# Value products of two heads issued alternately, and transpositions branch by branch, in a two-layer HGRN2 / NSA block

## The chip, the cores and the metric

One core of a Trainium2 chip runs the whole block in one launch. The metric is the device time of one execution in microseconds (us), the median of several runs; lower is better.

## The reference

The input x has 256 tokens of 1024 features. Layer 0 is an HGRN2 mixer and a gated feed-forward; layer 1 is a native sparse attention (NSA) mixer and another feed-forward, each with conditioning vectors (shift, scale, gate) made from c. The change touches the last step of the NSA mixer: for each head three softmaxes (compressed keys, selected blocks, window) are multiplied with their values, gated and added.

```python
p_c = masked_softmax(s_c, cmp_end[None, :] <= t[:, None])
o_c = jnp.einsum('bhgqc,bchd->bqhgd', p_c.astype(vc.dtype), vc)
...
p_s = masked_softmax(s_s, m_s[:, :, None])
o_s = jnp.einsum('bhgqk,bhqkd->bqhgd', p_s.astype(vs_g.dtype), vs_g)
...
p_w = masked_softmax(s_w, m_w)
o_w = jnp.einsum('bhgqk,bkhd->bqhgd', p_w.astype(vw.dtype), vw)
...
o = g[:, :, 0] * o_c + g[:, :, 1] * o_s + g[:, :, 2] * o_w
```

There are 16 query heads of 64 features on 4 key heads. With 256 tokens every block is selected and the window holds all earlier tokens, so selection and window are both causal attention over 256 keys, with keys and values of their own.

## The kernel before

All weights come as one stream of 1 MB chunks (`SCHED`, line 116), loaded by SP into a ring of four buffers (`raw`, lines 282 to 289). Most chunks are split into a high and a low fp32r part, `wh` on ACT and `wl` on DVE (lines 307 and 308), and each product is three matmuls of these parts (lines 484 to 486). Conditioning chunks are read by PE as they are (L385, tiles `adapsg` and `adapsss`).

The NSA stage works on eight column tiles j; a tile holds two heads, one on partitions 0 to 63 (half 0) and one on 64 to 127 (half 1). Tiles 0 to 3 belong to group g = 0, tiles 4 to 7 to g = 1. `attend_scores` (line 1195) makes scores on PE (`s`, L1207), adds the mask and takes maxima on DVE (L1211), exponentials on ACT (L429), reciprocals with gates on DVE (`cf`, L1223 to L1225), and scales the probabilities `Pt[half]` on DVE (L1229). For each half and each branch (br 0 selection, br 1 window) there are three blocks of 128 x 128: keys 0 with tokens 0, keys 0 with tokens 1, keys 1 with tokens 1.

`attend_values` (line 1233) transposes the three blocks of each half and branch on PE (`ptt`, L1244), copies them to SBUF (`PT[half, br]`; the first on DVE, L1247, the other three on ACT, L1249), and then sums the products with the values into one accumulator `po`. Half 0 writes its partitions 0 to 63 and half 1 its partitions 64 to 127, which are two column halves of the PE array (`tile_position=(0, 64 * half)`). For each half there are five products: compressed probabilities `PC` with `VC` over 256 tokens (L1256), and for each branch keys 0 over 256 tokens (L1260) and keys 1 over the last 128 (L1262). Before, all five of half 0 come first, then the five of half 1. Operands are plain fp32, and each such matmul is two instructions on the engine. At the end `split` (L479 on ACT, L480 on DVE) makes the parts `hh` and `hl` of the output projection's input (`nso`).

The same array halves are used by the compression products of line 1103 (tile `cmp`), which take the two kinds in turn, and the conditioning products of L385 use four column quarters.

The order of the work is `ORDER["nsa"]` (line 66): scores s, values v and conditioning chunks a are interleaved there. A tile scheduler then places the instructions by expected readiness and priority; `attend_values` is moved ahead by ten places (`@first("av")`, `PRI`). So the rows of one tile's step do not stand together in PE's queue, and other work stands between them. PSUM gives three buffers to `ptt` (tag `acc`, shared with the projections) and four to `po`, scores and others (tag `m`); `PT` has five buffers in SBUF.

Of the kernel before, what the change touches and what calls it, by code (L numbers as in the profile page):

```python
# [20 lines left out]
P = 128  # L21
S = 256
D = 1024
# [4 lines left out]
RAW = 4  # chunks loaded ahead  # L28
DEFER = 3  # chunks of a feed-forward's first product taken before rstd is there
XBUFS = 14  # L30
XMOD, XOFF = 5, 9  # every how many halves of a chunk go to the second ring, and until which chunk
PTS = 3  # pairs of heads with probabilities at a time
QACT, KACT = 0x0F, 0xF0  # chunks of the queries' and values' input made on ACT
CSTK = 7  # chunk after which the rest of the constants is loaded
# how far ahead of the program (behind it, if negative) some of the work is issued
PRI = {"gates": -100, "av": 10, "res": 60, "rot": -15, "fh": 60}
EPS = 1e-6
# [5 lines left out]


# conditioning vectors (s shift and scale, g gate) on the tensor engine; the others are row sums on DVE
# [11 lines left out]
# The order of the work. hgrn: D decays, S scores, i/g products, V values. nsa: q queries, G gates, c compression,  # L57
# n norms, w values, x compressed softmax, s scores, v outputs, a conditioning chunk.
# hada, f0, f1: after how many chunks of products each conditioning chunk comes.
# [115 lines left out]
def row_constants():  # L175
    """Row 32 m + h of column block m: ones on the partitions of half h."""
    r = np.zeros((P, 4, P), np.float32)
    for m in range(4):
        for h in range(2):
            r[32 * m + h, m, 64 * h:64 * h + 64] = 1.0  # L180
    return r.reshape(P, 4 * P)


def first(name):
    """What the method issues is moved by PRI in the order of the program."""
    def wrap(f):
        def g(self, *a, **k):
            n = PRI.get(name, 0)
            if not n:
                return f(self, *a, **k)  # L190
            with self.tc.high_priority(offset=n):
                return f(self, *a, **k)
        return g
    return wrap


class K:
# [154 lines left out]
    def ada(self, kind, l, i, t):  # L352
        """Two columns of 128 conditioning values: rows of the chunk against c."""
        nc = self.nc
        m, A, bias = self.ada_tiles(l)
        c0, c1 = (i, 8 + i) if kind == "ada_ss" else (16 + 2 * i, 17 + 2 * i)
        for h, c in enumerate((c0, c1)):
            junk = self.tp.tile([P, D], F32, tag="junk", bufs=1, name="junk")
            nc.vector.tensor_tensor_reduce(out=junk, in0=t[:, h * D:(h + 1) * D], in1=self.crep, scale=1.0,  # L359
                                           scalar=0.0, op0=ALU.mult, op1=ALU.add, accum_out=m[:, c:c + 1])  # L360
        if kind == "ada_ss":
            gain = self.col(self.gain(l))
            nc.vector.scalar_tensor_tensor(A[:, i:i + 1], m[:, c1:c1 + 1], self.bias1(l)[:, c1:c1 + 1],
                                           gain[:, i:i + 1], op0=ALU.add, op1=ALU.mult)
            nc.vector.tensor_tensor(m[:, i:i + 1], m[:, i:i + 1], bias[:, i:i + 1], op=ALU.add)
            if i == 7:
                self.mods[("A", l)] = A
                self.mods[("shift", l)] = m[:, 0:8]
        else:
            nc.vector.tensor_tensor(m[:, c0:c1 + 1], m[:, c0:c1 + 1], bias[:, c0:c1 + 1], op=ALU.add)  # L370
            if i == 3:
                self.mods[("gate", l)] = m[:, 16:24]

    def ada_pe(self, kind, l, i, t):
        """c against the chunk's rows, summed over the chunks; at the last one the columns."""
# [43 lines left out]
    def act(self, out, in_, func, **kw):  # L419
        """An activation whose function lies in a table set; sets change only between phases."""  # L420
# [17 lines left out]
    def rsqrt_cols(self, v, n, tag):  # L438
        """v ** -0.5 for a few columns, by Newton's method from the exponent."""
# [11 lines left out]
    def rsqrt(self, v, shape, tag):  # L451
        """(v + EPS) ** -0.5, one Newton step after the tables."""
# [13 lines left out]
    def sigmoid(self, out, v, shape):  # L466
        """exp(min(v, 0)) / (1 + exp(-|v|))"""
        nc = self.nc
        t = self.s2.tile(shape, F32, tag="sg", bufs=1, name="sg")
        nc.vector.tensor_scalar_min(t, v, 0.0)  # L470
        self.act(t, t, AF.Exp)
        nc.scalar.activation(out, v, AF.Abs)
        self.act(out, out, AF.Exp, scale=-1.0)
        nc.vector.tensor_scalar_add(out, out, 1.0)
        nc.vector.reciprocal(out, out)
        nc.vector.tensor_tensor(out, out, t, op=ALU.mult)
# [17 lines left out]
    def gemm(self, ps, w, hh, hl, n=256):  # L494
        """ps = sum over k of w[k] (128 x 128) against h[:, k, :n]."""
# [3 lines left out]
    def tiles(self, w):  # L499
        """The 128 x 128 tiles of half a chunk: high and low parts."""  # L500
# [7 lines left out]
    def set_shift(self, hh, hl, l):  # L508
        """Columns 256 and 257 of the moving operand: the shift vector and zeros."""
# [14 lines left out]
    def stat(self, x, m):  # L524
        """Adds the squares of chunk m to the sum over chunks."""
# [10 lines left out]
    def first_stat(self):  # L536
        """rstd of the input."""
# [25 lines left out]
    def stat_end(self, ps=None):  # L563
        """self.rstd = (mean of squares + EPS) ** -0.5 of every token, on all partitions."""
# [17 lines left out]
    def full_chunk(self, hh, hl, m, A, sh, pool):  # L582
        """Chunk m of x * rstd * A + shift, in two parts."""
# [7 lines left out]
    def full_pair(self, which, l, xr, pool, on_act):  # L591
        """The same from x * rstd."""
# [22 lines left out]
    def gemm_deferred(self, ws, h, pool, name, ub=2):  # L615
        """Products with h as it is before rstd: their values times rstd, and the shift's column."""
# [17 lines left out]
    def residual(self, ps, m, gate, nxt):  # L634
        """x_new chunk m = x + gate * y, with what the next products need of it."""
# [20 lines left out]
    def hgrn(self):  # L656
# [3 lines left out]
        with self.tc.tile_pool(name="hg", bufs=1) as gp, self.tc.tile_pool(name="hg2", bufs=2) as g2:  # L660
# [17 lines left out]
            # room of the next operands until their first parts are there  # L678
# [62 lines left out]
    def gemm_tok(self, ps, h, ws):  # L741
        """Tokens on the partitions: h (stationary) against the weights."""
# [9 lines left out]
    def hgrn_decays(self, fs, qs, g2):  # L752
        """X[l]: exp of the log decay from each block's middle; left keys, right queries. X[8]: keys."""
# [41 lines left out]
    def hgrn_scores(self, X, q, g2, i):  # L795
        nc = self.nc
        # scores inside blocks of 32, all levels side by side
# [45 lines left out]
    def hgrn_values(self, ns, As, v, g2, q):  # L843
        """Into q: rms-normalised rows of A^T v times the gain, features on the partitions."""
# [75 lines left out]
    def raw_heads(self, ps, name):  # L920
        """Products of two column tiles off the accumulator, and their squares."""
# [7 lines left out]
    def rotate(self, u, gain, swap, kr, name):  # L929
        """kr = the rotation of u times the gain: halves of a head change places."""  # L930
# [11 lines left out]
    def head_norm(self, pairs, kr, gain=None, kn=None):  # L942
        """Four column tiles: kr times the heads' rstd, kn = u times that and the gain."""
        nc = self.nc
        ps = self.m_tile([P, S], "hs")
        # rows 32 e and 32 e + 1: the two heads of column tile e
# [124 lines left out]
    def cmp_blocks(self, sw, u, kind, Dt, pool):  # L1071
        """Dt[(parity, d), i, (head, block)]: token 16 block + 2 i + parity of a head, plus its position."""
# [160 lines left out]
    def attend_values(self, j):  # L1233
# [4 lines left out]
        for half in range(2):  # L1238
            for br in range(2):
                PT[half, br] = self.pt_tile(f"PT{j}_{half}{br}")  # L1240
                pt = self.pp.tile([P, 3, P], F32, tag="acc", bufs=3, name="ptt")
                # columns: keys 0 with tokens 0, keys 0 with tokens 1, keys 1 with tokens 1
# [8 lines left out]
        for half in range(2):  # L1251
            hs = slice(64 * half, 64 * half + 64)
            kv = 2 * g + half
            o = po[hs]
            tpos = (0, 64 * half)
            nc.tensor.matmul(o, lhsT=self.VC[:, g, (j % 4) * 2 + half], rhs=self.PC[g].rearrange("p a b -> p (a b)"),  # L1256
                             start=True, stop=False, tile_position=tpos)
            for br in range(2):
                v = self.V[:, :, br, 64 * kv:64 * kv + 64]
                nc.tensor.matmul(o, lhsT=v[:, 0], rhs=PT[half, br][:, 0:S], start=False, stop=False,  # L1260
                                 tile_position=tpos)
                nc.tensor.matmul(o[:, P:S], lhsT=v[:, 1], rhs=PT[half, br][:, S:384], start=False, stop=br == 1,  # L1262
                                 tile_position=tpos)
# [6 lines left out]
def _kt(w):  # L1270
    """[K, M] -> [128, K / 128, M]"""
# [3 lines left out]
def head_order():  # L1275
    """Query heads by (column tile, half): halves of a tile use key heads 2 g and 2 g + 1."""
# [107 lines left out]
```

## Time and profile before

| what | us |
|---|---|
| median of 3 runs | 765.33 (764.39 to 766.17) |
| profiled execution: span, first to last instruction | 764.0 |
| median of the runs less that span | 1.3 |
| PE busy / weight loads / DVE / ACT, of the span | 736.8 / 671.6 / 573.1 / 395.2 |
| all transpositions, value products and what stands between them | 474 to 546 of the span |

The page gives for each engine the time in which it had at least one instruction under way. PE's matmuls overlap each other and their ends are modelled, so for PE the distance between the starts of two rows says what an instruction took. In a timeline, rows of one kind that follow each other are merged: start, length of the merged row, engine, line, operation, tiles, shape and count.

### The profile page before, as it was taken

What the parts mean: (1) busy time and instruction counts of PE and PEld (TensorE: products, weight loads), DVE (VectorE), ACT (ScalarE), POOL (GpSimd) and SP (SyncE); (2) the same over time, 40 slices, a digit from 0 to 9 for tenths busy, and PEclk for the clock granted to TensorE, in tenths of its full rate; (3) what the DMA queues carried; (4) which work ended last, traced back from release to release, by engine and by line L of the source; (5) the groups of instructions that cost most, each with busy time, mean ns of one, the idle gap of its engine ahead of it and who ended that gap; (6) DMA issues with size and microseconds to landing.
All of it is one profiled execution on the core that took longest, in us unless ns stands there. A gap on an engine that the chain in (4) does not pass through costs nothing.

```text
span 764.0 us, 15991 instructions
## 1 busy us (share of the span) xinstructions
PE 736.8 (96%) x6580; PEld 671.6 (88%) x6580; DVE 573.1 (75%) x1231; ACT 395.2 (52%) x746; POOL 0.6 (0%) x7
## 2 busy tenths in 40 slices
PE   3999999899999999999999899999999999999997
PEld 1999986689999999999996787555799999999997
DVE  5996988469898988987598869668489757565631
ACT  4339856357644544544474644558466444444330
POOL 0000000000000000000000000000000000000000
PEclk9999999799999999999999999999999999999999
DMA  8999745475489796887733942552755555755710
GB/s 330 335 341 355 274 133 210 139 284 203 143 320 377 275 366 266 333 333 285 274 112 97 359 134 74 173 215 109 275 204 182 208 179 206 275 203 205 266 39 21
DMA packets 26571, 174.13 MB, mean 228 GB/s; under 512 B 3201, under 2 KB 4609, under 8 KB 6018
## 3 DMA queue, kind: packets, MB, share of 16 engines
q1 hardware_dynamic: 24912, 170.80, 60.7%
q10 hardware_dynamic: 1586, 2.32, 1.1%
q8 instruction: 51, 0.84, 0.4%
q14 instruction: 22, 0.18, 0.1%
HBM read 170.48 MB, written 1.05 MB: 225 GB/s over the span
## 4 chain that ended last, share of the span: by engine, by line
PE 88%; DVE 5%; ACT 3%; DMA 2%; issue 1%; ACTq 0%; DVEq 0%
PE ff L486 11%; PE ff L485 11%; PE ff L484 11%; PE ffo L484 6%; PE ffo L485 5%; PE ffo L486 5%; PE adapsss L385 2%; PE po L1260 2%; PE ptt L1244 2%; PE s L1207 2%; DVE wl L308 1%; PE q L485 1%; PE nso L484 1%; PE hg_i L748 1%; PE hgo L484 1%; PE q L486 1%
## 5 line engine op out<-in xcount | busy, mean ns | idle before, releaser
L308 DVE TENSOR_TENSOR wl<-raw,wh 128x1024 fp32r<-128x1024 f32 x201 | 244.0, 1222 | 72.7 <-ACT wh L307 72.2
L307 ACT CAST wh<-raw 128x1024 fp32r<-128x1024 f32 x201 | 208.7, 1048 | 152.8 <-PE ff L485 53.0
L486 PE MATMUL ff<-hh,wl 128*128 128x256 f32 (+1 forms) x704 | 198.3, 282 | 0.0
L484 PE MATMUL ff<-hh,wh 128*128 128x256 f32 (+1 forms) x704 | 198.1, 282 | 0.0
L485 PE MATMUL ff<-hl,wh 128*128 128x256 f32 (+1 forms) x704 | 198.1, 282 | 0.0
L486 PEld LDWEIGHTS ff<-hh,wl 128*128 128x128 f32 x704 | 133.1, 189 | 0.0
L485 PEld LDWEIGHTS ff<-hl,wh 128*128 128x128 f32 x704 | 132.7, 189 | 0.3
L484 PEld LDWEIGHTS ff<-hh,wh 128*128 128x128 f32 x704 | 132.6, 189 | 0.1
L484 PE MATMUL ffo<-gh,wh 128*128 128x256 f32 x352 | 99.0, 282 | 0.6 <-DVE x L638 0.6
L485 PE MATMUL ffo<-gl,wh 128*128 128x256 f32 x352 | 98.6, 280 | 0.0
L486 PE MATMUL ffo<-gh,wl 128*128 128x256 f32 x352 | 98.5, 280 | 0.0
L359 DVE CUSTOM_DVE_ANT_0 junk<-raw,crep 128x1024 f32<-128x1024 f32 x64 | 78.1, 1220 | 2.8 <-DMA raw<-in_w 2.2
L484 PEld LDWEIGHTS ffo<-gh,wh 128*128 128x128 f32 x352 | 66.0, 188 | 1.3 <-DVE x L638 1.0
L486 PEld LDWEIGHTS ffo<-gh,wl 128*128 128x128 f32 x352 | 66.1, 188 | 0.0
L485 PEld LDWEIGHTS ffo<-gl,wh 128*128 128x128 f32 x352 | 66.1, 188 | 0.0
L479 ACT CAST gh<-fg 128x256 fp32r<-128x256 f32 x44 | 17.8, 405 | 42.0 <-DVE fg L894 41.4
L429 ACT ACTIVATE Pt<-Pt,nm 128x128 f32<-128x128 f32 x64 | 28.2, 442 | 9.8 <-DVE nm L1215 9.8
L480 DVE TENSOR_TENSOR gl<-fg,gh 128x256 fp32r<-128x256 f32 x44 | 18.6, 422 | 8.2 <-ACT gh L479 8.2
L587 ACT ACTIVATE hh<-t,mod 128x256 fp32r<-128x256 f32 x24 | 11.4, 505 | 24.6 <-DVE t L586 24.6
L429 ACT ACTIVATE fs<-ff 128x256 f32<-128x256 f32 x38 | 14.5, 380 | 15.3 <-PE ff L486 15.3
L638 DVE SCALAR_TENSOR_TENSOR x<-ffo,mod,x 128x256 f32<-128x256 f32 x16 | 7.7, 482 | 18.9 <-PE ffo L486 18.9
L385 PE MATMUL adapsss<-raw,c 128*32 128x512 f32 x128 | 21.1, 632 | 0.8 <-issue 0.8
(324 smaller groups left out, 1497.8 us busy)
## 6 DMA issues: line engine op xcount, KB each, us to landing
raw<-in_w SPq DMA_DIRECT2D x160, 1024.0 KB, 5.6
x<-in_x SPq DMA_DIRECT2D x2, 512.0 KB, 5.0
usq<-huq ACTq DMA_DIRECT2D x16, 64.0 KB, 2.4
out<-x SPq DMA_DIRECT2D x8, 128.0 KB, 1.9
cst<-in_cst ACTq DMA_DIRECT2D x1, 558.0 KB, 7.7
usk<-huk ACTq DMA_DIRECT2D x8, 64.0 KB, 3.9
raw<-in_w SPq DMA_DIRECT2D x1, 512.0 KB, 4.3
rselr<-in_rsel SPq DMA_DIRECT2D x1, 256.0 KB, 2.9
```

Source lines behind the costliest of these rows:

```text
L307: nc.scalar.copy(wh, u)
L308: nc.vector.tensor_tensor(wl, u, wh.bitcast(F32), op=ALU.subtract)
L359: nc.vector.tensor_tensor_reduce(out=junk, in0=t[:, h * D:(h + 1) * D], in1=self.crep, scale=1.0, scalar=0.0, op0=ALU.mult, op1=ALU.add, a ...
L385: nc.tensor.matmul(self.aps[32 * j:32 * j + 32, :q], lhsT=self.c32[:, k], rhs=t[:, n * D + j * q:n * D + (j + 1) * q], start=k == 0, stop= ...
L429: r = nc.scalar.activation(out, in_, func, **kw)
L479: self.nc.scalar.copy(hi, v)
L480: self.nc.vector.tensor_tensor(lo, v, hi.bitcast(F32), op=ALU.subtract)
L484: mm(ps, lhsT=wh, rhs=hh, start=first, stop=False)
L485: mm(ps, lhsT=wh, rhs=hl, start=False, stop=False)
L486: mm(ps, lhsT=wl, rhs=hh, start=False, stop=last)
L1207: nc.tensor.matmul(ps, lhsT=self.QR[hs, j, tt * P:tt * P + P], rhs=self.KR[hs, g, :, 0:n], start=True, stop=True)
L1244: nc.tensor.transpose(pt[:, e], Pt[half][:, br, e * P:(e + 1) * P], self.c("ident"))
```

## The change

The two nested loops over half and branch change places where the blocks are transposed: both halves of branch 0 first, then both of branch 1. And the ten value products go step by step, each step for half 0 and then half 1, in one statement (L1261 in the changed program, for L1256, L1260 and L1262 before). The first step opens the sum (`start`), the last closes it. The products themselves, their operands, shapes and places in the array are as before. The rest of the diff takes out comments and docstrings.

```diff
-        for half in range(2):
-            for br in range(2):
+        for br in range(2):
+            for half in range(2):
                 PT[half, br] = self.pt_tile(f"PT{j}_{half}{br}")
...
         po = self.m_tile([P, S], "po")
-        for half in range(2):
-            hs = slice(64 * half, 64 * half + 64)
-            kv = 2 * g + half
-            o = po[hs]
-            tpos = (0, 64 * half)
-            nc.tensor.matmul(o, lhsT=self.VC[:, g, (j % 4) * 2 + half], rhs=self.PC[g].rearrange("p a b -> p (a b)"),
-                             start=True, stop=False, tile_position=tpos)
-            for br in range(2):
-                v = self.V[:, :, br, 64 * kv:64 * kv + 64]
-                nc.tensor.matmul(o, lhsT=v[:, 0], rhs=PT[half, br][:, 0:S], start=False, stop=False,
-                                 tile_position=tpos)
-                nc.tensor.matmul(o[:, P:S], lhsT=v[:, 1], rhs=PT[half, br][:, S:384], start=False, stop=br == 1,
-                                 tile_position=tpos)
+
+        pc = self.PC[g].rearrange("p a b -> p (a b)")
+        steps = [(None, self.VC[:, g, (j % 4) * 2:(j % 4) * 2 + 2], pc, slice(0, S))]
+        for br in range(2):
+            for e, t in ((0, slice(0, S)), (1, slice(P, S))):
+                steps.append((br, self.V[:, e, br, P * g:P * g + P].rearrange("p (h d) -> p h d", h=2),
+                              slice(0, S) if e == 0 else slice(S, 384), t))
+        for n, (br, w, r, t) in enumerate(steps):
+            for half in range(2):
+                rhs = r if br is None else PT[half, br][:, r]
+                nc.tensor.matmul(po[64 * half:64 * half + 64, t], lhsT=w[:, half], rhs=rhs, start=n == 0,
+                                 stop=n == len(steps) - 1, tile_position=(0, 64 * half))
         self.split(self.O[0][:, j, :256], self.O[1][:, j, :256], po)
```

On PE, the block in which tile 2's products stand complete (tile 3's first ones ahead of them and among them). In `PT_01` the first digit is the half, the second the branch; 64x256 and 64x128 are what a product writes.

```order
-L1256 MATMUL po<-PC_5655,VC 64x256 x2
-L1260 MATMUL po<-PT_00_6249,V 64x256
-L1262 MATMUL po<-PT_00_6249,V 64x128
-L1260 MATMUL po<-PT_01_6255,V 64x256
-L1262 MATMUL po<-PT_01_6255,V 64x128
-L1256 MATMUL po<-PC_5655,VC 64x256
-L1260 MATMUL po<-PT_10_6261,V 64x256
-L1262 MATMUL po<-PT_10_6261,V 64x128
-L1260 MATMUL po<-PT_11_6267,V 64x256
-L1262 MATMUL po<-PT_11_6267,V 64x128
+L1261 MATMUL po<-PC_5655,VC 64x256 x4
+L1261 MATMUL po<-PT_00_6249,V 64x256
+L1261 MATMUL po<-PT_10_6255,V 64x256
+L1261 MATMUL po<-PT_00_6249,V 64x128
+L1261 MATMUL po<-PT_10_6255,V 64x128
+L1261 MATMUL po<-PT_01_6261,V 64x256
+L1261 MATMUL po<-PT_11_6267,V 64x256
+L1261 MATMUL po<-PT_01_6261,V 64x128
+L1261 MATMUL po<-PT_11_6267,V 64x128
```

Half 0 and half 1 now alternate row by row; tile 3's product of half 1 with `PC` came to this block from the next one. Of the four rows with `PC` the first two are half 0 of tiles 2 and 3, the last two half 1.

Also on PE, in the changed program, the products of tile 6 and the last transpositions of tile 7 (`Pt_0_6557` and `Pt_1_6558`, halves 0 and 1), with the numbers of the buffers:

```order
L1261 MATMUL po_6627<-PT6_00_6603,V_4885 64x256
L385 MATMUL adapsss3_6426<-raw117_6437,c32_110 32x512 x3
L385 MATMUL adapsss3_6426<-raw118_6601,c32_110 32x512 x4
L385 MATMUL adapsss3_6426<-raw119_6644,c32_110 32x512 x4
L1261 MATMUL po_6688<-PC1_6382,VC_5474 64x256
L1261 MATMUL po_6627<-PT6_10_6609,V_4885 64x256
L1261 MATMUL po_6627<-PT6_00_6603,V_4885 64x128
L1244 MATMUL ptt_6665<-cst_80,Pt7_0_6557 128x128
L1261 MATMUL po_6627<-PT6_10_6609,V_4885 64x128
L1261 MATMUL po_6627<-PT6_01_6615,V_4885 64x256
L1244 MATMUL ptt_6665<-cst_80,Pt7_0_6557 128x128 x2
L1261 MATMUL po_6627<-PT6_11_6621,V_4885 64x256
```

Here the scheduler has put other work between the two halves of a step: `PT6_00` stands alone ahead of eleven conditioning products, and `PT6_01` is parted from `PT6_11` by transpositions.

On ACT, the copies of tile 1 among the steps of the query norm (`hry`, `hrt`):

```order
 L1249 COPY PT_11_6065<-ptt 128x384
-L1249 COPY PT_01_6090<-ptt 128x384
+L1249 COPY PT_10_6090<-ptt 128x384
 L429 ACTIVATE hry<-hry 128x256
-L1249 COPY PT_10_6096<-ptt 128x384
+L1249 COPY PT_01_6096<-ptt 128x384
+L459 ACTIVATE hrt<-hry 128x256
 L1249 COPY PT_11_6102<-ptt 128x384
-L459 ACTIVATE hrt<-hry 128x256
```

The two middle copies carry the other pair of half and branch, and the square `hrt` now goes before the last copy of tile 1.

## Rows read from the trace of the kernel before

**Rows 1.** From the page: the span, and the shares of the chain that ended last by engine.

```profile
span 764.0 us, 15991 instructions
...
PE 88%; DVE 5%; ACT 3%; DMA 2%; issue 1%; ACTq 0%; DVEq 0%
```

**Rows 2.** Busy time by stretch: stretch and its length, then busy us and instructions of PE, weight loads, DVE, ACT and POOL, the granted clock of PE, the share of the DMA engines, GB/s.

```profile
475.00:546.00 71.00, 70.49 (x459) 39.22 (x460) 46.56 (x209) 40.72 (x140) 0.00 (x0) 1.00 0.50 189
546.00:600.00 54.00, 53.80 (x443) 53.09 (x444) 46.38 (x88) 33.76 (x61) 0.00 (x0) 1.00 0.54 185
```

**Rows 3.** The chain of waits in the window 460 to 560 us: shares of this window by engine, tile and line (the row is cut by the view).

```profile
by line: PE po L1260 14.3%; PE ptt L1244 13.3%; PE s L1207 12.3%; PE adapsss L385 9.5%; ACT Pt L429 7.1%; PE po L1262 6.5%; PE po L1256 6.0%; PE nso L484 5.1%; PE nso L486 4.6%; PE nso L485 4.5%; PE adapsg L385 3.4%; DVE Pt L1211 2.4%; PE c
```

**Rows 4.** The matmuls that write the tile `po`: count, durations (least, median, most, in ns), first and last start, form (the part of the array, the moving operand).

```profile
L1260 PE MATMUL po<-PT,V x64: 379/379/430, 479.6 to 545.3; 128*64 128x256 f32 x64
L1262 PE MATMUL po<-PT,V x64: 272/273/323, 480.1 to 545.6; 128*64 128x128 f32 x64
L1256 PE MATMUL po<-PC,VC x32: 379/379/431, 475.9 to 544.2; 128*64 128x256 f32 x32
```

**Rows 5.** The timeline of PE from 497.4 to 501.0: the block of the first listing above.

```profile
497.48 1.08 PE L1256 MATMUL po<-PC,VC 128*64 128x256 f32 x4
498.40 0.59 PE L1260 MATMUL po<-PT,V 128*64 128x256 f32 x2
498.83 0.38 PE L1262 MATMUL po<-PT,V 128*64 128x128 f32 x2
499.05 0.38 PE L1260 MATMUL po<-PT,V 128*64 128x256 f32 x1
499.05 0.43 PE L1256 MATMUL po<-PC,VC 128*64 128x256 f32 x1
...
499.48 0.27 PE L1262 MATMUL po<-PT,V 128*64 128x128 f32 x1
...
500.19 0.59 PE L1260 MATMUL po<-PT,V 128*64 128x256 f32 x2
500.62 0.38 PE L1262 MATMUL po<-PT,V 128*64 128x128 f32 x2
500.93 0.44 PE L396 MATMUL adat<-cst,adasm 128*128 128x128 f32 x2
```

**Rows 6.** The timeline of the compression products, 416.2 to 424: weight loads and matmuls.

```profile
416.32 6.67 PEld L1103 LDWEIGHTS cmp<-raw,D 128*64 128x64 f32 x62
416.32 7.12 PE L1103 MATMUL cmp<-raw,D 128*64 128x256 f32 x62
```

**Rows 7.** The timeline of PE from 473 to 547: where blocks of products and their neighbours begin.

```profile
479.60 0.65 PE L1260 MATMUL po<-PT,V 128*64 128x256 f32 x2
...
481.53 1.91 PE L385 MATMUL adapsg<-raw,c 128*32 128x256 f32 x26
...
484.18 0.65 PE L1260 MATMUL po<-PT,V 128*64 128x256 f32 x2
...
487.41 1.20 PE L1244 MATMUL ptt<-cst,Pt 128*128 128x128 f32 x9
488.55 1.07 PE L385 MATMUL adapsg<-raw,c 128*32 128x256 f32 x16
489.55 0.51 PE L959 MATMUL hb<-hry,rsel 128*128 128x256 f32 x2
...
506.61 0.65 PE L1260 MATMUL po<-PT,V 128*64 128x256 f32 x2
...
509.19 1.20 PE L1244 MATMUL ptt<-cst,Pt 128*128 128x128 f32 x9
```

**Rows 8.** Groups of instructions on ACT, 475 to 546: count, busy us, mean ns of one, idle time before them and what ended it.

```profile
L429 ACT ACTIVATE Pt<-Pt,nm 128x128 f32<-128x128 f32 (+1 forms) x48 | 21.1, 443 | 4.8 <-DVE nm L1215 4.8
...
L1249 ACT COPY PT<-ptt 128x384 f32<-128x384 f32 x24 | 10.5, 478 | 11.1 <-PE ptt L1244 10.5 <-ACT wh L307 0.6
```

**Rows 9.** Who waited for whom, 475 to 546: us in total, times, longest.

```profile
ACT PT L1249 <- PE ptt L1244: 10.5, 7, 4.6
ACT hh L479 <- PE po L1262: 9.6, 5, 3.1
...
DVE Pt L1211 <- PE s L1207: 3.1, 5, 1.1
...
PEld ptt L1244 <- DVE cf L1223: 1.6, 2, 0.8
```

**Rows 10.** The same view, 546 to the end.

```profile
ACT wh L307 <- PE ff L485: 34.1, 25, 1.8
```

**Rows 11.** Busy time by stretch, columns as in rows 2.

```profile
520.00:525.00 5.00, 5.00 (x20) 2.10 (x19) 4.59 (x25) 5.00 (x24) 0.00 (x0) 1.00 0.13 51
530.00:535.00 5.00, 5.00 (x35) 2.34 (x37) 4.58 (x12) 4.96 (x21) 0.00 (x0) 1.00 0.00 0
```

**Rows 12.** The same view, ahead of the stage of the change.

```profile
405.00:410.00 5.00, 3.30 (x17) 2.46 (x18) 5.00 (x10) 2.00 (x5) 0.00 (x0) 0.83 0.22 41
410.00:415.00 5.00, 5.00 (x36) 4.87 (x36) 4.17 (x13) 2.62 (x8) 0.00 (x0) 0.83 0.69 236
445.00:450.00 5.00, 3.27 (x25) 3.06 (x24) 4.96 (x13) 2.17 (x3) 0.00 (x0) 0.92 0.01 3
450.00:455.00 5.00, 5.00 (x34) 5.00 (x34) 4.36 (x6) 1.05 (x2) 0.00 (x0) 0.74 0.60 202
```

## The prediction

> **What bounds the kernel now.** I read the head of the page first: the span is 764.0 us and TensorE (PE) makes 88% of the chain of work that ended last [rows 1]. So an edit is worth what it takes off PE's queue in a stretch where PE is the chain. The edit touches only the products `po` and the transpositions `ptt`, which stand between 475 and 546 us; the busy time by stretch shows PE taken for 70.5 of those 71 us at full clock (1.00 in the clock column is the 2.4 GHz level), with DVE at 47 and ACT at 41 [rows 2]. A busy PE in this profile may still be a slow PE, since its matmuls overlap, so I went on to the chain of waits of the window 460 to 560. That window is 100 us long, so a per cent is a microsecond: the three lines of the products hold 14.3 + 6.5 + 6.0 = **26.8 us** [rows 3]. They are 160 instructions (each matmul of the program with fp32 operands is two on the engine): 96 over 256 columns and 64 over 128 [rows 4].
>
> **What such a product costs.** The timeline of one block, tiles 2 and 3, shows it [rows 5]. Distances between starts are what counts; the durations in the rows overlap. Four products of one half start at 497.48 and the next group at 498.40: 0.92 us, which is 4 x 0.216 and 0.05 for the change of the array's shape. Two over 128 columns take 499.05 - 498.83 = 0.22, so 0.109 each. The last two start at 500.62 and the next work, of another shape, at 500.93: 0.31, two times 0.109 and 0.09 for the change back. A piece of products between other work thus costs its stream and 0.05 + 0.09, some 0.15.
>
> At 499.05 two rows start together: L1260 of half 0 and L1256 of half 1. They write different column halves of the array and run side by side. The kernel has a stage that does this all along: the compression products of L1103 are issued alternately for column halves 0 and 64, and 62 of them take 7.12 us [rows 6]; the last one's own 0.38 taken off, that is 61 steps in 6.74 us, 0.110 each, half of 0.216. It is the same shape (128 rows, 64 columns, 256 moving columns, fp32). So **two halves side by side cost as much as one**, and the edit makes the products stand in that order.
>
> Here a rule of the Trainium skill speaks against the change: "TensorE: Matmul & The Clock Gate", Part 3, says that a load of weights overlaps a matmul in flight only where the two use different rows of the array, and that matmuls start strictly in program order. Both halves here use all 128 rows, so by it alternation would win nothing (rival 2). The trace disagrees: 62 loads go beside 62 products in the compression [rows 6], and L1256 at 499.05 started ahead of L1262 at 499.48, which the program issues before it.
>
> **Products, after.** Not every second can be won, since the halves overlap in part already and a scheduler places the rows. In the order of the program before, half 1's first product stands four engine instructions behind the place where it started [rows 5], so I let a product start as soon as the one four places ahead has started, and its own half is free. One row of the order is 0.43 us (256 columns) or 0.22 (128). Down the order of the changed program, stream and 0.15 for each piece:
> - Tiles 0 and 1: twice two rows of the same half, 1.01 each; then 00, 10, 00, 10, 01: 0.43 + 0.22 + 0.43 + 0.15 = 1.23; then eleven rows, half 1 the longer with 1.95: 2.10.
> - Tiles 2 and 3: twelve rows, all in pairs: 2.16 + 0.15 = 2.31; then eight in pairs: 1.45.
> - Tiles 4 and 5: 1.01, 1.01, 0.58, 0.37 (scores and transpositions stand between), ten rows 1.87, four 0.79, and a single one, 0.58.
> - Tiles 6 and 7: 0.58, 0.79, 0.58, 0.58, 0.37, 0.58, 0.58, and seven rows 1.45.
>
> These 21 pieces are 20.8 us. Before, the same stretch has the 26.8 of the chain; as a check on the method, the pieces of tiles 0 to 3 before take 1.93 (479.60 to 481.53), 3.23 (484.18 to 487.41), 3.45 (497.48 to 500.93) and 2.58 (506.61 to 509.19) [rows 5, 7], against 1.23, 2.10, 2.31 and 1.45 now. **Products: -6.0 us.**
>
> **The transpositions.** Their number stays, as does that of the copies to SBUF, 24 of them on ACT [rows 8], the others on DVE. Nine take 488.55 - 487.41 = 1.14 [rows 7], 9 x 0.109 and 0.15 for the piece. The order has one piece fewer: -0.15, bounds 0 and -0.3. Branch by branch, half 1's first copy is needed by the second product instead of the fifth. What hides that is the distance: the transpositions stand in the order ahead of the products of the tile before. I found one place where it is thin, tile 1: an activation of the query norm now goes before that tile's last copy on ACT. The nearest rows are an exp of 0.44 and a copy of 0.48 [rows 8]; bounds 0 and 0.5, and I take +0.3, nearer the exp, since the wait is for one such instruction less the slack of the products ahead.
>
> **The conditioning products.** Their eight rows of one chunk were one piece; two of them now come later, behind products. A whole chunk takes 489.55 - 488.55 = 1.00, four steps of 0.216 deep [rows 7]. The torn chunk adds two steps at most (0.43) and nothing at least; I take +0.35, since the six rows left still go four deep.
>
> **What does not move.** DVE's order changes by one pair of rows, ACT's copies change names (half 1 before branch 1) and three neighbours change places, SP's and POOL's queues are as before, so no DMA is issued in another place. The weight chunks follow PE: buffers come free when PE has read them. Behind the stage, PE stays taken for 53.8 of 54 us [rows 2], and the casts of weights wait for PE (34.1 us on the first feed-forward line alone) [rows 10], not PE for them; a stage that ends earlier therefore ends the kernel earlier by as much.
>
> **Sum.** -6.0 - 0.15 + 0.3 + 0.35 = -5.5 us, against the profiled execution's 764.0: 758.5. The median of the runs, 765.33, lies 1.3 above that span; I carry this along: **759.8 us**.
>
> **Rivals.**
> 1. *The gain is half given back to the softmax.* Between 520 and 535 ACT is full (5.00 and 4.96 of 5 us) and DVE nearly (4.59, 4.58) [rows 11]: exps and scales of tiles 5 to 7 could become the chain there, and PE would wait for probabilities. For it: PE already waited 1.6 us for DVE's reciprocals [rows 9]. Against it: ACT waited 10.5 us for transpositions and 9.6 for `po`, DVE 3.1 for scores [rows 9], so their work moves up with PE. What tiles 0 to 3 win stays: 1.01 + 1.93 + 3.23 + 3.45 + 2.58 = 12.2 becomes 9.1 + 0.3, -2.8, less 0.35 and with 0.15: 762.7 us.
> 2. *No gain that shows.* Products over 128 columns and mixed accumulations do not pair as the compression does, or all of the gain is eaten: 765.3. Nothing in the trace shows two 128-column products side by side; if these alone did not pair, 30 pairs of 0.109 would go, 3.3 us, and 763.1 would remain. Against that: transpositions load 128 columns of weights every 0.109 us, so two loads of 64 fit [rows 7]. Or the halves never run together: a load of weights waits for the other half's product because both use all 128 rows. That too gives 765.3, with a chance of 0.01 within this rival's; it is the Trainium skill's rule above, and the loads beside products in the compression speak against it [rows 6].
> 3. *Slower: PE runs into gaps and the clock falls.* The clock column fell in this kernel after stretches in which PE was taken for 3.30 and 3.27 of 5 us: 0.83 and 0.83, then 0.92 and 0.74 [rows 12]. Each time some 1.7 us of full-speed work was lost ((0.17 + 0.17) x 5, (0.08 + 0.26) x 5), beside the 1.7 us of idle time: 3.4 us. The place is the same, a product that stands at the head of PE's queue while its copy is queued on ACT behind eight exps (8 x 0.44 = 3.5 us), between 520 and 535. One such gap leaves a gain of 2.1; two decide: -5.5 + 6.8 = +1.3, 766.6 us. Against it: ACT's copies keep their places among the exps.
> 4. *More than I count.* Products reach further ahead than four places, and small waits of `ptt` vanish (1.6 us in the waits): 757.8.
>
> **Chances.** The forecast 0.74 (its own range 758.3 to 761.3), rival 1 and the 128-column case 0.10, rival 2 in full 0.07, rival 3 0.04, rival 4 0.05. The range takes the forecast, rival 4 and rival 1: 757.5 to 763.5. A measurement of this kernel can tell about 0.2%, 1.5 us, from no change: forecast, rivals 1 and 4 are faster by more, 0.89; the same 0.07; slower 0.04.
>
> **What would show it.** After the change, the three lines' share of the chain should be some 21 us; the block of tiles 2 and 3 should last 2.3 us instead of 3.45, with starts in pairs some 0.01 us apart; the first `nso` product should start near 540.3 instead of 545.8; the distance from there to the end should be as before. A piece of products as long as before, with alternating rows, would prove the pairing wrong; `ptt` or `po` with idle time before them and ACT's copies as releaser would prove rival 1; a clock below 1.00 between 475 and 541 rival 3.

## The result, and the profile after

The changed kernel took **759.21 us** (median of 20 runs, 754.96 to 760.88), the kernel before 764.66 (20 runs, 759.40 to 766.17). The two medians differ by 5.45 us. The ratio of the runs is 0.9926, with a 95% interval of 0.9914 to 0.9939; of 764.66 that is 5.66 us less, 4.7 to 6.6. The forecast was 759.8 us, and a difference of -5.5.

The page of the changed kernel, its span and the shares of the chain by engine, beside [rows 1]:

```profile
span 759.1 us, 15984 instructions
...
PE 88%; DVE 5%; ACT 3%; DMA 2%; issue 1%; ACTq 0%; DVEq 0%
```

PE still sets the time, and the span is 4.9 us shorter. The chain of waits from 460 to 560, as in [rows 3]:

```profile
by line: PE po L1261 21.2%; PE ptt L1244 12.9%; PE s L1207 12.3%; PE adapsss L385 9.5%; ACT Pt L429 7.1%; PE nso L484 6.8%; PE nso L485 6.2%; PE nso L486 6.0%; PE adapsg L385 4.8%; DVE Pt L1211 2.4%; PE cs L1172 1.7%; PE adat L396 1.1%; PE 
```

The three lines of the products, 26.8 us, are one line with 21.2. Transpositions went from 13.3 to 12.9, the conditioning products `adapsg` from 3.4 to 4.8 by this view; scores `s`, `adapsss` and ACT's exps are as they were. The instructions are the same ones, with the same durations as in [rows 4]:

```profile
L1261 PE MATMUL po<-PT,V x128: 272/352/430, 481.1 to 540.8; 128*64 128x256 f32 x64, 128*64 128x128 f32 x64
L1261 PE MATMUL po<-PC,VC x32: 379/379/431, 476.4 to 537.8; 128*64 128x256 f32 x32
```

So no product became shorter; they start closer together. The timeline of the block of tiles 2 and 3, for [rows 5]:

```profile
497.94 1.09 PE L1261 MATMUL po<-PC,VC 128*64 128x256 f32 x8
498.85 1.48 PE L1261 MATMUL po<-PT,V 128*64 128x256 f32 x16
500.26 0.44 PE L396 MATMUL adat<-cst,adasm 128*128 128x128 f32 x2
```

Eight products take 0.91 us from 497.94 to the next group; before, four took 0.92. The block of 24 lasts 500.26 - 497.94 = 2.32 us; before, a block of 22 took 3.45. Where the two products of a pair read different tiles, the timeline lists them apart and shows the pairs themselves (here around 518 us):

```profile
518.34 0.43 PE L1261 MATMUL po<-PC,VC 128*64 128x256 f32 x1
518.36 0.43 PE L1261 MATMUL po<-PT,V 128*64 128x256 f32 x1
518.61 0.38 PE L1261 MATMUL po<-PC,VC 128*64 128x256 f32 x1
518.62 0.38 PE L1261 MATMUL po<-PT,V 128*64 128x256 f32 x1
```

Starts lie 0.01 to 0.02 apart, and the next pair comes 0.26 to 0.27 later (in a block, 0.216). That products over 128 columns pair as well is read from the second block of tiles 2 and 3:

```profile
505.94 1.56 PE L1261 MATMUL po<-PT,V 128*64 128x256 f32 x16
507.43 1.20 PE L1244 MATMUL ptt<-cst,Pt 128*128 128x128 f32 x9
```

It has eight products of each width and takes 1.49 us. One after the other they would take 2.60 and 0.15 for the piece, with the wide ones alone in pairs 1.88, all in pairs 1.45.

The stretches, columns as in [rows 2] and [rows 11]:

```profile
475.00:540.50 65.50, 65.01 (x461) 34.24 (x460) 45.83 (x213) 41.40 (x141) 0.00 (x0) 1.00 0.51 191
540.50:600.00 59.50, 59.36 (x489) 58.40 (x486) 50.48 (x93) 36.09 (x64) 0.00 (x0) 1.00 0.56 198
520.00:525.00 5.00, 5.00 (x30) 2.69 (x30) 3.87 (x21) 3.97 (x16) 0.00 (x0) 1.00 0.02 5
530.00:535.00 5.00, 5.00 (x37) 1.66 (x35) 3.06 (x13) 3.57 (x11) 0.00 (x0) 1.00 0.46 134
```

PE is taken for 65.01 of the 65.50 us, at a granted clock of 1.00. The work of the stage begins with the first score product and is over with the first `nso` product; the first two lines are of the kernel before, the last two of the changed one:

```profile
463.69 0.49 PE L1207 MATMUL s<-KR,QR 64*128 64x256 f32 x2
...
545.83 0.39 PE L484 MATMUL nso<-hh,wh 128*128 128x256 f32 x1
...
464.26 2.48 PE L1207 MATMUL s<-KR,QR 64*128 64x256 f32 x12
...
540.98 0.38 PE L484 MATMUL nso<-hh,wh 128*128 128x256 f32 x1
```

That is 540.98 - 464.26 = 76.72 us; before it was 545.83 - 463.69 = 82.15 (from times with three digits, which the lines round). From the first `nso` product to PE's last matmul it is 214.48, before 214.52.

**How the experiments are read.** In all profiles here the first score product starts between 460.6 and 464.3 us, though PE's order up to it is the same: that part differs from execution to execution, and the medians carry it. The stage from that product to the first `nso` product doesn't: a second profile of the change gave 76.72 again. So the tables of the experiments give both, and the stage decides where it can. "Products" is the sum, over the value products of the stage, of the distance from each one's start to the next start on PE; a piece is a row of value products with no other work of PE between them. Each median stands against that of the kernel before, run beside it.

| kernel | stage, us | against before | products | pieces | median against before (95%) |
|---|---|---|---|---|---|
| before | 82.15 | | 26.83 | 20 | |
| the change | 76.72 | -5.43 | 21.20 | 21 | -5.66 (-6.6 to -4.7) |
| alternating products alone | 77.93 | -4.22 | 22.12 | 22 | -4.1 (-5.7 to -2.7) |
| transpositions alone | 81.49 | -0.66 | 26.19 | 20 | -1.45 (-2.7 to -0.2) |
| same column half | 96.37 | +14.22 | 31.98 | 24 | +11.6 (+10.4 to +12.8) |
| by twos | 75.88 | -6.27 | 20.91 | 20 | -7.3 (-8.6 to -6.1) |
| tied | 79.50 | -2.65 | 21.64 | 13 | -4.3 (-5.8 to -2.7) |
| by threes | 75.82 | -6.33 | 20.97 | 18 | -6.3 (-8.3 to -4.1) |

### The profile page after: what moved, and what is told of

Same layout as the page of the kernel before. It is cut to its first block, busy times and chain, and to the rows that moved or that the text cites. A ratio compares the mean times of both kernels' runs of the same rounds, so it can differ in the third digit from the quotient of the medians.

```text
span 759.1 us, 15984 instructions
## 1 busy us (share of the span) xinstructions
PE 731.4 (96%) x6580; PEld 665.8 (88%) x6580; DVE 572.9 (75%) x1231; ACT 395.7 (52%) x746; POOL 0.6 (0%) x7
## 3 DMA queue, kind: packets, MB, share of 16 engines
q10 hardware_dynamic: 1586, 2.32, 1.1%
## 4 chain that ended last, share of the span: by engine, by line
PE 88%; DVE 5%; ACT 3%; DMA 2%; issue 1%; ACTq 0%; DVEq 0%
PE ff L486 11%; PE ff L485 11%; PE ff L484 11%; PE ffo L484 5%; PE ffo L485 5%; PE ffo L486 5%; PE po L1261 3%; PE adapsss L385 2%; PE ptt L1244 2%; DVE wl L308 2%; PE s L1207 2%; PE q L485 1%; PE adapsg L385 1%; PE q L486 1%; PE nso L484 1%
## 5 line engine op out<-in xcount | busy, mean ns | idle before, releaser
L1211 DVE CUSTOM_DVE_ANT_0 Pt<-s,cst 128x128 f32<-128x128 f32 (+1 forms) x64 | 19.0, 350 | 2.9 <-PE s L1207 2.9
```

The costliest lines, as they stand in the source:

```text
L1211: nc.vector.tensor_tensor_reduce(out=Pt[half][:, br, o:o + n], in0=ps[:, br], in1=cs[:, S - n:], scale=1.0, scalar=-3e38, op0=ALU.add, op1 ...
```

## The experiments

Theory A: products of the two column halves run side by side, and the new order lets each find its partner within PE's reach. Theory B: the gain comes from the order of the transpositions and from where the scheduler then puts things. Theory C: alternation helps whatever columns are used, because a product needn't wait for the sum that the one ahead adds to. Theory D: only neighbours in the order pair.

**1. The alternating products alone.** The change without its new transposition order:

```diff
-        for br in range(2):
-            for half in range(2):
+        for half in range(2):
+            for br in range(2):
                 PT[half, br] = self.pt_tile(f"PT{j}_{half}{br}")
```

> The alternating products alone; the transpositions go half by half as before the change. Theory A (products of the two column halves run side by side, and the order of the program lets them): nearly the whole gain stays, -4.8 us against the kernel before (the pieces of products sum to 21.9 us instead of 26.8; the transpositions 13.6 to 14.5). Theory B (the gain is the order of the transpositions, which bring half 1's copy early, and the new places that the scheduler finds): -1 us or less of a gain, products at 25 us or more.

760.40 us beside 765.03, ratio 0.9946 (0.9926 to 0.9965). The stage lost 4.22 us, with 22.12 of products and 14.34 of transpositions. Theory A; B is out. The -4.8 that was expected came 0.6 short: products took 0.2 more than counted, and conditioning products 0.4 more than before. The block of tiles 2 and 3 is the change's, 0.91 for the eight products:

```profile
496.16 1.09 PE L1261 MATMUL po<-PC,VC 128*64 128x256 f32 x8
497.07 1.48 PE L1261 MATMUL po<-PT,V 128*64 128x256 f32 x16
```

**2. The transpositions alone.** The kernel before with its two transposition loops exchanged (the same diff the other way round), products as before.

> The transpositions branch by branch alone; the products stand as before the change, all of half 0 and then all of half 1. Theory A: -0.65 us against the kernel before, which a measurement can hardly tell from nothing; products 26.1 us. Theory B: most of the gain, -4 us or more.

763.24 us beside 765.03, ratio 0.9981 (0.9965 to 0.9997). The stage lost 0.66 us, 0.64 of it in the products (26.19), as Theory A had it. The products of the block stay unpaired for their first 1.56 us (494.43 to 495.99):

```profile
494.43 1.08 PE L1256 MATMUL po<-PC,VC 128*64 128x256 f32 x4
495.34 0.59 PE L1260 MATMUL po<-PT,V 128*64 128x256 f32 x2
495.77 0.38 PE L1262 MATMUL po<-PT,V 128*64 128x128 f32 x2
495.99 0.38 PE L1260 MATMUL po<-PT,V 128*64 128x256 f32 x1
496.00 0.43 PE L1256 MATMUL po<-PC,VC 128*64 128x256 f32 x1
...
496.43 0.27 PE L1262 MATMUL po<-PT,V 128*64 128x128 f32 x1
...
497.88 0.44 PE L396 MATMUL adat<-cst,adasm 128*128 128x128 f32 x2
```

3.45 us, to the hundredth what it was before. Alone the two parts give -4.22 and -0.66, together -5.43: the other 0.55 comes only when both are there. Which rows bring it was not traced.

**3. The same column half.** The order of the change, but both halves use columns 0 to 63 of the array.

```diff
+        po1 = self.m_tile([P, S], "po")
...
-                nc.tensor.matmul(po[64 * half:64 * half + 64, t], ..., tile_position=(0, 64 * half))
-        self.split(self.O[0][:, j, :256], self.O[1][:, j, :256], po)
+                nc.tensor.matmul((po, po1)[half][0:64, t], ..., tile_position=(0, 0))
+        for half in range(2):
+            hs = slice(64 * half, 64 * half + 64)
+            self.split(self.O[0][hs, j, :256], self.O[1][hs, j, :256], (po, po1)[half][0:64])
```

> The order of the change, but the products of both halves use the same column half of the array: half 1 goes to partitions 0 to 63 of a second PSUM tile. Left different: half 1's outputs land on the wrong partitions, and the split into hi and lo parts is made per half (8 more instructions each on ACT and DVE). Theory A: nothing pairs, each row of products takes its own stream, so products take 28 to 30 us instead of 21, starts 0.216 us apart and never 0.01; 8 to 14 us slower than the change's forecast place, that is +3 to +14 against the kernel before. Theory C (alternation alone helps, since a product that adds to the same PSUM region as the one ahead has to wait for it, whatever columns are used): products stay near 21 to 23 us and the time stays 3 us or more below the kernel before.

776.37 us beside 765.03, ratio 1.0151 (1.0136 to 1.0167). Products take 31.98 us; no two of the 160 start within 0.09 us of each other (49 such pairs of neighbours within 0.03 in the change). 96 x 0.216 + 64 x 0.109 + 24 x 0.15 = 31.3 is what they cost one by one, so the 28 to 30 that was expected left out the pieces. Theory C falls: alternation alone pairs nothing. In this run both halves also write the same PSUM partitions, so it does not tell the columns of the array from the partitions that they write to. The stage lost more than the products, and the timeline shows to what:

```profile
532.58 1.05 PE L385 MATMUL adapsss<-raw,c 128*32 128x512 f32 x2
533.55 0.65 PE L1262 MATMUL po<-PC,VC 128*64 128x256 f32 x2
534.13 1.05 PE L385 MATMUL adapsss<-raw,c 128*32 128x512 f32 x2
535.10 0.65 PE L1262 MATMUL po<-PC,VC 128*64 128x256 f32 x2
```

Here the scheduler laid conditioning products two by two between the others; a pair takes 533.55 - 532.58 = 0.97 us. A piece of eight takes 1.00 in the same profile. All 64 take 18.50 us, 9.50 in the kernel before: they too live off running side by side, four column quarters at a time, and lose it when torn. +5.15 of products and +9.00 of these make up all but 0.07 of the stage's +14.22. The spans of the two profiles differ by 11.7 only, because the stretch ahead of the stage is 2.5 us shorter in this one; why it was shorter is not known.

**4 and 5. By twos.** The two products of a branch (256 and 128 columns) stay together for a half, so equal products stand four instructions apart in PE's order instead of two.

```diff
-        for n, (br, w, r, t) in enumerate(steps):
+        for grp in ((0,), (1, 2), (3, 4)):
             for half in range(2):
-                ...
+                for n in grp:
+                    br, w, r, t = steps[n]
+                    ...
```

> The change with the products grouped: the step of the compressed branch for both halves, then the two steps (256 and 128 columns) of the selected branch for half 0 and for half 1, then the same for the window. Equal rows of the two halves now stand four instructions of the engine apart instead of two. Theory A with the look-ahead of four places that the forecast used: pairing stays whole, products 20.6 us, 20 pieces and no wait at tile 1: -6.9 us against the kernel before, about 1 below the change. Theory D (only neighbours pair, a look-ahead of two): the pairs within each branch go, products 24 us or more, and the time is 2 us or more above the change's.

758.08 us beside 765.03, ratio 0.9904 (0.9888 to 0.9920); stage -6.27, products 20.91 in 20 pieces. Theory D is out: with a reach of two the products would have been 24 or more. By the stage it was expected 0.6 better than it came (products 20.6, and 20.91 were measured); by the median, -7.3, it came 0.4 better. Beside the change on one chip:

> The products by twos once more, beside the change on the same chip. Theory A (the look-ahead of four places holds, and grouping saves one piece of products, the wait at tile 1 and the torn conditioning chunk): 0.9 us below the change, 6.4 below the kernel before. Rival (the first run's lead of 1.1 us over the change was the difference of two sessions): within 0.3 us of the change.

758.04 us, ratio 0.9907 (0.9883 to 0.9930), stage 75.88 again. And the change itself:

> The changed kernel itself, beside the products by twos: 5.5 us below the kernel before by the forecast's sum, with 21.2 us of products and the first nso product 66.4 us behind the first transposition, as in its first profile.

759.57 us, ratio 0.9925 (0.9906 to 0.9944), stage 76.72. The two intervals overlap, so the times alone don't separate the two; the stage does, by 0.84 us, with both kernels profiled twice; so the rival's 0.3 us does not fit. Its parts: products -0.3, transpositions -0.15 (13.99), `adapsg` -0.40 (4.41: the conditioning chunk is whole again). By the stage, by twos is the better order of the two.

**6. Tied.** The first product of a tile may not be put ahead of the tile's last transposition.

```diff
-                    nc.tensor.transpose(pt[:, e], ...)
+                    last = nc.tensor.transpose(pt[:, e], ...)
...
-                nc.tensor.matmul(po[64 * half:64 * half + 64, t], ...)
+                m = nc.tensor.matmul(po[64 * half:64 * half + 64, t], ...)
+                if n == 0:
+                    self.after(m, last)
```

> The change with each tile's first product tied behind that tile's last transposition in PE's order, so that the products fall into 13 pieces instead of 21. It tests the price of 0.15 us for a piece, and what the scattered places hide. If 0.15 is right, the products' own rows take 1.2 us less than the change's 21.2 less its wait of 0.3, that is 19.7 us where nothing waits. What it costs is waits: PE comes to products and transpositions sooner than their copies on ACT and DVE (2.7 us at tile 6, and some of 0.4 to 1.1), so that the stage gains nothing or loses up to 1 us: 4.5 to 5.5 us below the kernel before, all told -4.9. Rival (a piece costs nothing, the 0.15 is only the overlap of two shapes): the products stay at 20.5 us or more without waits, and the time is 1 us or more above the change's.

760.48 us beside 764.94, ratio 0.9944 (0.9924 to 0.9965): -4.3 by the median, just outside the 4.5 to 5.5 that were expected, and only -2.65 in the stage of the one execution that was profiled. The expectation missed in both directions. The products are 21.64 us, and one piece of them holds a wait:

```profile
527.32 0.65 PE L1261 MATMUL po<-PC,VC 128*64 128x256 f32 x4
527.80 1.27 PE L1261 MATMUL po<-PT,V 128*64 128x256 f32 x10
531.86 0.98 PE L1261 MATMUL po<-PT,V 128*64 128x256 f32 x6 [2.79 <-ACT PT L1249]
532.78 0.48 PE L1244 MATMUL ptt<-cst,Pt 128*128 128x128 f32 x1
```

That piece takes 5.45 us; the other three pieces of twenty products take 1.88 or 1.89. Without the 3.57 us above that, products are 18.1, not 19.7: eight pieces fewer save 2.8 us against the change's 20.9 without its wait, 0.35 a piece. The rival, that a piece costs nothing, falls. The 0.15 for the change of shape held in the change's pieces (below); the rest goes with more products finding a partner (60 neighbours start within 0.03 us of each other here, 49 in the change), though no run holds the two apart. The wait's length, 2.7, was right too. What was not counted is its consequence:

```profile
527.00:532.00 5.00, 2.21 (x19) 1.19 (x20) 4.68 (x11) 4.32 (x19) 0.00 (x0) 1.00 0.40 115
532.00:537.00 5.00, 4.64 (x23) 3.02 (x22) 2.64 (x10) 2.82 (x5) 0.00 (x0) 0.66 0.76 301
537.00:542.00 5.00, 5.00 (x36) 3.59 (x36) 1.03 (x5) 0.38 (x1) 0.00 (x0) 1.00 0.02 7
```

PE was taken for 2.21 of 5 us, and then the granted clock fell to 0.66 for 5 us: 5 x 0.34 = 1.7 us of full-speed work, a part of the stretch at the lower level, 1.2 GHz. Transpositions took 17.26 us instead of 14.14, with waits and that clock in them; scores took 1.4 us less. Whether the clock fell in the other executions of this kernel is not known.

**7. By threes.** Groups of three and two products, so that equal products of the first group stand six instructions apart: `for grp in ((0, 1, 2), (3, 4))` in the diff of 4.

> The products in two groups: compressed branch and selected branch (three products, six instructions of the engine) for half 0, then for half 1; then the window (two products, four instructions) for each half. Equal rows of the halves stand six places apart in the first group. With the look-ahead of four, half 1 starts two instructions late in each first group and the pairing is lost at its ends only: products 20.8 to 21.0 us, 18 pieces, the stage from the first score to the first nso product 76.4 (the change 76.7, by twos 75.9), 5.8 below the kernel before. Rival (a look-ahead without a limit): 75.9 or less, no worse than by twos. Rival (no reach beyond four places at all, so a group of six runs alone before the other half may start): products 23 us or more, 78.5 or more.

757.91 us beside 763.90, ratio 0.9918 (0.9891 to 0.9946). Stage 75.82, products 20.97 in 18 pieces. The products are as expected; the stage came 0.6 below and meets the bound of the rival without a limit, so the total doesn't tell the two apart. The block does:

```profile
494.23 1.08 PE L1263 MATMUL po<-PC,VC 128*64 128x256 f32 x4
495.14 0.38 PE L1263 MATMUL po<-PT,V 128*64 128x256 f32 x1
495.15 0.43 PE L1263 MATMUL po<-PC,VC 128*64 128x256 f32 x1
...
497.02 0.44 PE L396 MATMUL adat<-cst,adasm 128*128 128x128 f32 x2
```

Four products run alone for 0.91 us before the other half joins, and 22 take 2.80 us. By twos, 24 take 2.36:

```profile
495.46 1.09 PE L1263 MATMUL po<-PC,VC 128*64 128x256 f32 x8
496.37 1.52 PE L1263 MATMUL po<-PT,V 128*64 128x256 f32 x16
497.82 0.44 PE L396 MATMUL adat<-cst,adasm 128*128 128x128 f32 x2
```

So the reach ends: four places are covered, at six a block pays about 0.4 us (the two blocks of tiles 2 and 3 take 2.80 + 1.89 us by threes, 2.36 + 1.50 by twos, for 40 products each), at ten (before: 3.45 + 2.58) about 1.1. In all, by threes has 20.97 us of products in two pieces fewer, by twos 20.91: a draw.

## Why the prediction was right

**The bound.** PE was the chain and stays it. What came off the stage came off the end: 5.43 us in the stage, 214.5 us behind it before and after. The first `nso` product starts at 540.98 and not near 540.3, since the stage began 0.57 us later in this execution.

**Products: -6.0 + 0.3 forecast, -5.63 measured** (26.83 to 21.20). Of the 21 counted pieces, 20 came within 0.05 us of the count, among them: tiles 2 and 3 2.31 and 1.45, measured 2.32 and 1.49 (505.94 to 507.43); tiles 4 and 5 1.87 and 0.79, measured 1.88 and 0.80; tiles 0 and 1 1.23, measured 1.23. The price of 0.216, of 0.109 and of 0.15 for a piece held, and products over 128 columns pair like the others. Theory A was shown from three sides: alone it gives 4.22 (experiment 1), with both halves on the same columns it is gone (experiment 3), and its reach is at least four places (experiment 4).

**The wait at tile 1: +0.3 forecast.** The piece counted at 2.10 took 2.45 (485.44 to 487.89). In it PE's weight loads wait for ACT:

```profile
485.65 0.42 ACT L459 ACTIVATE hrt<-hry 128x256 f32<-128x256 f32 x1
486.34 0.48 ACT L1249 COPY PT<-ptt 128x384 f32<-128x384 f32 x1 [0.27 <-PE po L1261]
...
486.87 0.20 PEld L1261 LDWEIGHTS po<-PT,V 128*64 128x64 f32 x4 [0.16 <-ACT PT L1249]
```

The weight loads stand idle for 0.16 us; of the 0.35 the rest is not traced further. The size came out, the reason did not. The forecast had the square `hrt` hold up the copy, but `hrt` was done at 486.07, and the copy then stood idle for 0.27 us until a product (L1261) let it go. Such a wait fits a copy that needs one of the five buffers of `PT` which that product still read; this is argued from the program, not shown. That this term came out is luck.

**Transpositions: -0.15 forecast, -0.31 measured** (14.45 to 14.14 by the distances between starts), at the bound that was given. **The torn conditioning chunk: +0.35 forecast, +0.25 measured** (`adapsg` 4.56 to 4.81). Not counted were +0.15 for the transpositions `adat` and +0.11 for `hs`, which lie in one piece more. -5.63 - 0.31 + 0.25 + 0.15 + 0.11 = -5.43, against -5.5. So the products carry the result, and the small terms miss by -0.16, -0.10 and +0.26, which cancel: that the sum agrees to 0.1 us is in part luck.

**Rival 1** (the softmax becomes the chain) didn't come. ACT is still full, in other stretches than those of [rows 11], and PE stays taken there:

```profile
524.00:529.00 5.00, 5.00 (x43) 3.17 (x41) 4.59 (x20) 5.00 (x15) 0.00 (x0) 1.00 0.00 0
```

But it is not the chain: in the two chains of 460 to 560, `ACT Pt` holds 7.1 and `DVE Pt` 2.4 before and after. PE's matmuls wait for ACT once between 475 and 541, for 0.5 us, as before, and ACT waits for PE as in [rows 9]:

```profile
PE ptt L1244 <- ACT V L1032: 0.5, 1, 0.5
ACT PT L1249 <- PE ptt L1244: 10.8, 7, 4.6
```

**Rival 2** (no pairing) is refuted by the starts. The rule of the Trainium skill ("TensorE: Matmul & The Clock Gate", Part 3) that a load of weights overlaps a matmul only where the two use different rows of the array, and that matmuls start in the order of the program, taken by itself as the prediction took it, doesn't describe these runs: both halves use all 128 rows and start 0.01 to 0.02 us apart, and in experiment 2 the L1256 of half 1 at 496.00 starts ahead of the L1262 at 496.43, which the program issues before it.

**Rival 3** (gaps, then a lower clock) didn't come in the change, whose stage ran at 1.00. Its mechanism was seen once: the execution of experiment 6 has the gap at the place that the rival named, a product at the head of PE's queue while its copy waits on ACT between 520 and 535, with 2.79 us of idle time and 1.7 us of clock. The change itself has no such gap. **Rival 4** (a longer reach) is out: products, 21.20, came within 0.1 us of the count with four places and the wait (20.8 + 0.3), and experiment 7 shows the reach end short of six.

**The total.** The 0.6 us between 759.8 and 759.21 are not from the change: the forecast started from a median of 3 runs, 765.33, and over 20 runs the kernel before has 764.66.

## What to carry to other kernels

In this kernel two series of fp32 matmuls, each on its own 64 columns of the array, ran side by side when equal products stood two or four instructions apart in PE's order: two instructions over 256 columns then took 0.216 us, as one alone does. At six apart a part of that was lost, and at ten about half (26.83 us of products before, 21.20 in the change, 31.98 where nothing pairs). Read it from the starts, not the durations, which were the same before and after. And an order that gathers small work into larger pieces is only worth its savings if PE doesn't reach a copy before it is made: in experiment 6 the idle time came with a loss of clock on top.

## What the runs showed of the hardware

- Column quarters run side by side too: in the profile of experiment 3, two, four, six or eight conditioning products (32 columns of the array, 512 moving columns) between other work take 0.98, 0.98, 0.99 and 1.00 us.
- Eight pieces fewer saved 2.8 us of products in the tied order, 0.35 each; 0.15 of that is the stream's break by itself (0.05 and 0.09 at its two ends), the rest goes with more pairs.
- In the profiled execution of the tied order, one gap of 2.79 us on PE was followed by a granted clock of 0.66 over 5 us, although PE was taken for 4.64 of these.
- The same order of the same work ahead of the stage takes 460.6 to 464.3 us from one execution to the next; the stage itself repeats to 0.01 us.
